# Seven block products in place of eight for the second FFN's input, and its width in three parts

## The chip, the cores and the metric

The kernel runs on one core of a Trainium2 chip. TensorE (PE) multiplies, VectorE (DVE) and ScalarE (ACT) do elementwise work, GpSimd (POOL) a few small operations, and SyncE (SP) issues the weight transfers. Each engine works through its own instructions in program order, and semaphores order the engines against each other. The metric is the device time of one execution in microseconds (us).

## The reference, cut to what matters

Two transformer blocks run one after the other on a sequence of 256 tokens with 2048 channels, in float32. What the change touches is the second block's feed-forward network, of width 5632:

```python
def conv_ffn(h, w_ffn_in, conv_w, conv_b, w_ffn_out):
    S = h.shape[1]
    up = h @ w_ffn_in                               # 2048 x 11264
    a, b = up[..., :D_FF_2], up[..., D_FF_2:]       # D_FF_2 = 5632
    a_pad = jnp.pad(a, ((0, 0), (CONV_W - 1, 0), (0, 0)))
    a = (conv_w[0] * a_pad[:, 0:S] + conv_w[1] * a_pad[:, 1:S + 1]
         + conv_w[2] * a_pad[:, 2:S + 2] + conv_b)
    return (jax.nn.gelu(a, approximate=True) * b) @ w_ffn_out
```

The input h is the RMS-normed row, and the output gets an RMS norm of its own and is added to x. The first block has a gated network of the same width (silu(g) * u), without the convolution.

## The kernel before, in words

**Products.** Each float32 weight and activation is split in two parts, high and low (`hi`, `lo`), and a product is three matmuls: high by high, high by low, low by high. A weight block is 128 x 1024: two contraction tiles of 128 by one group of 512 columns. `Sched` streams the blocks in one fixed order through all stages: SP loads a block into one of 4 raw buffers (`wraw`, L92), ACT writes its high part (`whi`, L113), DVE the low part (`wlo`, L115), each into one of 5 buffers. `take` hands the next block to PE; it first loads up to 6 blocks ahead (`LEAD_DMA`) and splits up to 4 ahead (`LEAD_SPLIT`). `q.tick()` follows each block and runs what was put off by a number of ticks (`later`, `step_of`) and a step of the background work (`q.work`).

**V tasks.** A group of 512 output columns takes 8 blocks of 12 matmuls with 512 moving columns (L1261 to L1263): 96 matmuls. The second FFN's input before is such tasks alone: group j of the convolved half, then group 11+j of the other half, for j from 0 to 10. We call the two a pair, of 192 matmuls. The first one (`by_tile`) runs the two halves of the tokens one after the other. Each group is evacuated by `f2_evac`: ACT scales the two accumulators into `ab`; two ticks later PE transposes 8 blocks of 128 x 128 (L465) into two PSUM tiles `m`. For the convolved half `conv` follows on each tile (two ACT operations at L1107, four of DVE through the helper at L283, then `gelu` on ACT); for the other half `gated` multiplies on DVE and `act_split` writes the high part on ACT and the low part on DVE.

**S tasks.** The first FFN's input runs in pairs already (`pairs_of_groups`, `pair_products`, products in the helper `three`, L1286 to L1288). Eight contraction pairs c are gone through in the order `ORDER`. Five of them take their two blocks as they are, 24 matmuls. For the three in `SEVEN` a 2 x 2 block product is formed with 7 products in place of 8 (21 matmuls): their blocks go out as left, sums1, sums2, right. The two sums blocks are made by DVE from the left and the right raw block with four operations (L145 to L149) and split like any other, so the raw buffers of both stay taken until then. The sums of the activations (`comb`) are made once beforehand, by `combine`. At the last of the sevens DVE builds four partial results from the four extra PSUM tiles (`u`, `g`), and each of the accumulators is added to one of them.

**Order and space.** All is written in program order by `Sched`; no planner reorders it. Activations, `hx4`, `x1`, `ff`, `act` and others live in 15 slots of 8 KB per partition (`slot`). The second FFN's width is worked through in the two parts of `PARTS`: groups 0 to 5, then 6 to 10. After each part the output product `w_f2o` (V tasks) adds that part's share to `ff` in `f_out`; in the last part group 3 of the output is run by the task `W` with 256 moving columns, in two halves, and the end of it is the end of the kernel: `f_tile`, `out_row`, and the stores.

Of the kernel before, what the change touches and what calls it, by code (L numbers as in the profile page):

```python
# [19 lines left out]
S = 256  # L20
# [6 lines left out]
PARTS = ((0, 6), (6, NG))  # L27
A_HEADS = 8
# [200 lines left out]
def body(ctx, tc, A, out):  # L229
# [149 lines left out]
    def pairs_of_groups(arr, of, order, lhs, comb, gate, done, first):  # L379

        blks = [b for x, y in of for b in pair_blocks(arr, x, y, order)]
        tasks.append(("S", blks, (len(of), order, lhs, comb, gate, done, first)))
# [4 lines left out]
    st = {}  # L387
# [79 lines left out]
    def turned(key, f0, srcs, use=None, then=None, gain=None, wait=2, comb=()):  # L467

        def part(j):
            def fn():  # L470
                m = mtile()
# [22 lines left out]
    def combine(key, i, m, gain):  # L494

        y, s = t512("y"), t512("s4")
        for n in range(2):
            copy(y[:, cols(n, S)], m[:, cols(n, S)], gain[n])
        a11, a21, a12, a22 = [y[:, cols(n, P)] for n in range(4)]
# [7 lines left out]
        halves(st[("comb", key)][i // 2][:, i % 2], s)  # L507

# [263 lines left out]

    for a, b in PARTS:
        C(lambda n=b - a: new_h("act", n))
        pairs_of_groups(A["w_f1"], [(j, NG + j) for j in range(a, b)], ORDER, rhs_of("hx2"), comb_of("hx2"), n1, "act",
                        (b - a) % 2)
# [352 lines left out]
    def f2_evac(key, j, use, then):  # L1129
        def evac(accs):  # L1130
            turned(key, 4 * j, scaled("ab", accs, n3), use, then)
        return evac

# [7 lines left out]
    def f_out(g, part):  # L1141
        def evac(accs):
            for k in range(2):
                y = st["ff"][k][:, cols(g)]
                if part == 0:
                    copy(y, accs[k])
                else:
                    out_sum(accs[k], k, g, cols(g))
            if part:
# [38 lines left out]
    def start_ff():  # L1188
        st["ff"] = [slot([P, D], name="ff") for _ in range(2)]
        st["post"] = slot([P, D], name="post")  # L1190
# [99 lines left out]
    def turn_act(key, f0, rows, tile):  # L1290
        for j in range(2):
            m = tile()
            turn(m, rows, j)
            f = f0 + 2 * j
            h_tile(key, f)
            dst = st[key][f // 4][:, f % 4:f % 4 + 2]
            split(dst[:, :, 0], dst[:, :, 1], pairs(m))

    def pair_products(count, order, lhs, comb, norm, key, first):
# [4 lines left out]
        prev = None  # L1304
        for n in range(count):
            own, shared = (acc_tile, mtile) if (n + first) % 2 == 0 else (mtile, acc_tile)
            for i, (c, seven) in enumerate(order):
# [30 lines left out]
                else:  # L1338
# [29 lines left out]
        turned(key, 4 * (count - 1), prev)  # L1368

# [112 lines left out]
def _layout(a):  # L1482
# [28 lines left out]
    r["w_f2os"] = _wblk(a["w_ffn_out_2"][0], range(4 * PARTS[1][0], 4 * NG))  # L1511
# [20 lines left out]
```

## Time and profile before

| what | value |
|---|---|
| time, median of 3 runs | 2739.64 us (2739.2 to 2743.42) |
| profiled execution, its own time | 2742.58 us |
| its span, first to last instruction | 2740.8 us |
| busy: PE, DVE, ACT | 2708.5 us (99%), 1689.7 us (62%), 1355.4 us (49%) |
| first FFN's input, S tasks | 851 to 1110 us and 1275 to 1460 us |
| second FFN's input, V tasks | about 1984 to 2265 us and 2396 to 2623 us |

Times inside the profile are us from the start of the span. A PE matmul's shown duration overlaps with the next one, so what a matmul costs is the distance from its start to the start of the next, and a busy PE need not be PE at its peak. Idle time stands in brackets ahead of what ended it.

### The profile page before, as it was taken

Reading aid. Unit: us, or ns where it says so; the run is one execution under the profiler, and the core shown is the slowest. Engines: PE = TensorE matmul, PEld = TensorE weight load, DVE = VectorE, ACT = ScalarE, POOL = GpSimd, SP = SyncE. Lnnn points to the kernel's source line nnn. Section 1 sums busy time; section 2 is a strip of 40 time slices with the busy share of each in tenths; the row PEclk is TensorE's granted clock in tenths of the full one; section 3 lists DMA queues with packets and bytes.
Section 4 is the critical chain, followed back from the end, with each engine's and each line's share of the span. In section 5 each row is a group of like instructions: output and inputs, shape, how many; then the busy total and the mean of one; then the engine's idle time right before and its main releaser. Section 6 shows DMA issues by size and latency. Waiting matters only on the chain.

```text
span 2740.8 us, 33567 instructions
## 1 busy us (share of the span) xinstructions
PE 2708.5 (99%) x12777; PEld 2253.2 (82%) x12777; DVE 1689.7 (62%) x2033; ACT 1355.4 (49%) x1759; POOL 59.5 (2%) x61
## 2 busy tenths in 40 slices
PE   8999999999999999999999999999999999999998
PEld 7888788888888887888888888888778888888887
DVE  5456555554467898648886557775555554455555
ACT  5445444444455555435555455554455554455543
POOL 0000000000000000000000001110000000000000
PEclk9999999999999999999999999999999999999999
DMA  8554456555555555655656565445555555555554
GB/s 276 175 181 163 160 171 215 194 189 196 191 177 195 179 200 191 209 194 182 207 184 204 183 210 168 145 152 191 177 177 184 185 185 191 192 191 185 185 189 142
DMA packets 142227, 511.42 MB, mean 187 GB/s; under 512 B 16945, under 2 KB 17329, under 8 KB 141553
## 3 DMA queue, kind: packets, MB, share of 16 engines
q1 hardware_dynamic: 140832, 502.71, 55.6%
q0 software_dynamic: 1088, 6.55, 0.6%
q8 instruction: 100, 1.64, 0.2%
q14 instruction: 63, 0.51, 0.1%
q10 hardware_dynamic: 144, 0.01, 0.0%
HBM read 507.11 MB, written 2.10 MB: 186 GB/s over the span
## 4 chain that ended last, share of the span: by engine, by line
PE 82%; DVE 8%; DMA 4%; issue 3%; ACT 2%; POOL 0%; DVEq 0%; ACTq 0%; POOLq 0%
PE acc L1263 21%; PE acc L1261 21%; PE acc L1262 21%; PE acc L1388 8%; DVE wlo L115 4%; PE acc L1390 4%; DMA wraw<-in_w_f 3%; PE m L465 1%; ACT whi L113 1%; DVE u L277 1%; PE acc L1286 1%; PE acc L1287 1%; PE acc L1288 1%; DVE sums L145 1%; DVE sums L146 1%
## 5 line engine op out<-in xcount | busy, mean ns | idle before, releaser
L115 DVE TENSOR_TENSOR wlo<-wraw,whi 128x1024 fp32r<-128x1024 f32 (+1 forms) x934 | 1119.3, 1206 | 802.6 <-ACT whi L113 798.7
L113 ACT ACTIVATE whi<-wraw 128x1024 fp32r<-128x1024 f32 (+1 forms) x934 | 966.6, 1041 | 788.3 <-PE acc L1263 675.0
L1261 PE MATMUL acc<-whi,hx 128*128 128x512 f32 x1456 | 581.7, 400 | 7.1 <-ACT hx L274 5.3
L1262 PE MATMUL acc<-wlo,hx 128*128 128x512 f32 x1456 | 568.4, 390 | 1.2 <-DVE wlo L115 1.2
L1263 PE MATMUL acc<-whi,hx 128*128 128x512 f32 x1456 | 569.3, 391 | 0.0
L1388 PE MATMUL acc<-hx,whi 128*128 128x512 f32 x912 | 330.6, 404 | 0.0
L1261 PEld LDWEIGHTS acc<-whi,hx 128*128 128x128 f32 x1456 | 274.0, 188 | 64.3 <-ACT hx L274 5.3
L1262 PEld LDWEIGHTS acc<-wlo,hx 128*128 128x128 f32 x1456 | 274.2, 188 | 58.8 <-DVE wlo L115 2.4
L1263 PEld LDWEIGHTS acc<-whi,hx 128*128 128x128 f32 x1456 | 273.8, 188 | 58.5
L1261 PE MATMUL acc<-whi,act 128*128 128x512 f32 (+1 forms) x704 | 271.1, 385 | 0.0
L1263 PE MATMUL acc<-whi,act 128*128 128x512 f32 (+1 forms) x704 | 269.8, 383 | 0.0
L1262 PE MATMUL acc<-wlo,act 128*128 128x512 f32 (+1 forms) x704 | 269.8, 383 | 0.0
L1390 PE MATMUL acc<-hx,wlo 128*128 128x256 f32 x912 | 255.7, 280 | 0.0
L1388 PEld LDWEIGHTS acc<-hx,whi 128*128 128x128 f32 x912 | 171.3, 188 | 38.9 <-issue 0.5
L1390 PEld LDWEIGHTS acc<-hx,wlo 128*128 128x128 f32 x912 | 172.4, 189 | 1.0 <-issue 0.5
L1263 PEld LDWEIGHTS acc<-whi,act 128*128 128x128 f32 x704 | 132.3, 188 | 26.1
L1261 PEld LDWEIGHTS acc<-whi,act 128*128 128x128 f32 x704 | 132.3, 188 | 25.7
L1262 PEld LDWEIGHTS acc<-wlo,act 128*128 128x128 f32 x704 | 132.4, 188 | 25.4
L113 ACT ACTIVATE whi<-sums 128x1024 fp32r<-128x1024 f32 x66 | 68.9, 1057 | 112.6 <-DVE sums L146 72.9
L1286 PE MATMUL m<-whi,hx 128*128 128x512 f32 x291 | 113.8, 391 | 0.0
L1288 PE MATMUL m<-whi,hx 128*128 128x512 f32 x291 | 113.3, 389 | 0.0
L1287 PE MATMUL m<-wlo,hx 128*128 128x512 f32 x291 | 113.3, 389 | 0.0
(332 smaller groups left out, 3047.9 us busy)
## 6 DMA issues: line engine op xcount, KB each, us to landing
wraw<-in_w_f SPq DMA_DIRECT2D x352, 512.0 KB, 3.4
wraw<-in_w_f1o SPq DMA_DIRECT2D x88, 512.0 KB, 4.2
wraw<-in_w_f2o SPq DMA_DIRECT2D x78, 512.0 KB, 3.3
wraw<-in_w_ga SPq DMA_DIRECT2D x34, 512.0 KB, 3.3
wraw<-in_w_vr SPq DMA_DIRECT2D x32, 512.0 KB, 3.3
wraw<-in_w_gr SPq DMA_DIRECT2D x32, 512.0 KB, 3.3
wraw<-in_w_gret SPq DMA_DIRECT2D x32, 512.0 KB, 3.9
wraw<-in_w_or SPq DMA_DIRECT2D x32, 512.0 KB, 3.3
```

The lines of the kernel that those rows point to most:

```text
L113: nc.scalar.activation(hi[:, c], raw[:, c], AF.Copy)
L115: nc.vector.tensor_tensor(lo[:, c], raw[:, c], hi[:, c].bitcast(F32), op=ALU.subtract)
L145: tt(t1, b12, b11, op=ALU.subtract)
L146: tt(t3, b22, b12, op=ALU.subtract)
L1261: nc.tensor.matmul(accs[k], x[:, 0], hi[:, w], start=b, stop=False)
L1262: nc.tensor.matmul(accs[k], x[:, 0], lo[:, w], start=False, stop=False)
L1263: nc.tensor.matmul(accs[k], x[:, 1], hi[:, w], start=False, stop=e)
L1286: nc.tensor.matmul(acc, x[:, 0], hi, start=start, stop=False)
L1287: nc.tensor.matmul(acc, x[:, 0], lo, start=False, stop=False)
L1288: nc.tensor.matmul(acc, x[:, 1], hi, start=False, stop=stop)
L1388: nc.tensor.matmul(acc, hi[:, w], x.rearrange("p a b -> p (a b)"), start=(k == first), stop=False, skip_group_check=True)
L1390: nc.tensor.matmul(acc[:, S:], lo[:, w], x[:, 0], start=False, stop=(k == last), skip_group_check=True)
```

## The change

The second FFN's input becomes S tasks too, for ten of its eleven pairs; pair 0 stays as two V tasks. A new order `ORDER_2` places the three sevens at 3, 5 and 6 of 8, the last two next to each other. `hx4` is not kept unsplit, so `combine_later` adds its two halves again and forms the sums, one step per tick, starting in the second V task of pair 0. What follows a pair is put into classes: `Gated` for the first FFN does what stood in `pair_products` before, except that the last pair's transposes go into the accumulators' own PSUM tiles; `Convolved` adds the accumulators to the partial results on DVE (`rows`), scales on ACT, and calls `turned` with `conv` or `gated` as before. The width is worked through in three parts (`PARTS_2`: groups 0 to 3, 4 to 7, 8 to 10), so `f_out` runs once more and the task `W` has 12 contraction tiles in place of 20, with its `out_row` calls placed anew. `ffn_post_norm_2` is loaded ahead of the last part's output and not of the first's. The sums slot of the first FFN is given back after it (`free_sums`).

```diff
+PARTS_2 = ((0, 4), (4, 8), (8, NG))
...
+    def combine_later(key, cs):
+        for i, c in enumerate(cs):
+            y = t512("y")
+            x = st[key][c // 2][:, 2 * c % 4:2 * c % 4 + 2].bitcast(F32)
+            tt(pairs(y), x[:, :, 0], x[:, :, 1], ALU.add)
+            yield
+            sums_of(key, i, y)
+            yield
...
+    class Convolved:
+        def last(self, n, shared):
+            pass
+
+        def rows(self, accs, y):
+            for k in range(2):
+                tt(y[k], accs[k], y[k], ALU.add)
+            for k in range(2):
+                copy(y[k], y[k], n3.r[:, k:k + 1])
+
+        def left(self, n, accs, g, own):
+            self.rows(accs, g)
+            turned("conv", 4 * (self.j0 + n), g, conv(self.f0), gelu, tile=own)
+
+        def right(self, n, accs, u, own):
+            self.rows(accs, u)
+            turned("act", 4 * (self.j0 + n), u, gated, act_split, tile=own)
...
+    ORDER_2 = [(3, False), (4, False), (0, True), (5, False), (1, True), (2, True), (6, False), (7, False)]
+    end = PARTS_2[-1][0]
-    for a, b in PARTS:
+    for a, b in PARTS_2:
         C(lambda n=b - a: (new_h("act", n), new_h("conv", 0)))
-        for j in range(a, b):
-            if j:
-                V(A["w_f2"], j, hx4, f2_evac("conv", j - a, conv(4 * a), gelu))
-            else:
-                by_tile(A["w_f2"], 0, hx4, first_tile, x4_hooks)
-            V(A["w_f2"], NG + j, hx4, f2_evac("act", j - a, gated, act_split))
         if a == 0:
-            C(start_ff)
-        for g in range(4 if a == 0 else 3):
+            by_tile(A["w_f2"], 0, hx4, first_tile, x4_hooks)
+            C(lambda: q.work[0].append(combine_later("hx4", SEVEN)))
+            V(A["w_f2"], NG, hx4, f2_evac("act", 0, gated, act_split, acc_tile))
+        js = range(max(a, 1), b)
+        pairs_of_groups(A["w_f2"], [(j, NG + j) for j in js], ORDER_2, hx4, comb_of("hx4"),
+                        Convolved(4 * a, js[0] - a), len(js) % 2)
+        C(start_ff if a == 0 else load_post if a == end else lambda: None)
+        for g in range(4 if a < end else 3):
             V(A["w_f2o"], g, lambda k, a=a: rhs_of("act", 5)(k - 4 * a), f_out(g, a), cs=range(2 * a, 2 * b))
-    W(A["w_f2os"], range(4 * PARTS[1][0], 4 * NG), lambda k: act_row(k - 4 * PARTS[1][0]), f_last, f_tile,
-      {(1, g): [(out_row, 0, g)] for g in range(4)})
+    W(A["w_f2os"], range(4 * end, 4 * NG), lambda k: act_row(k - 4 * end), f_last, f_tile,
+      {(1, 0): [(out_row, 0, 0)], (1, 1): [(out_row, 0, 1), (out_row, 0, 2)], (1, 2): [(out_row, 0, 3)]})
```

In `pair_products` the code after the last block of a pair's left and right half becomes:

```diff
                     if e:
-                        if prev is not None:
-                            turn_act(key, 4 * (n - 1), prev, shared)
-                        for k, acc in enumerate((c11, c21)):
-                            tt(g[k], acc, g[k], ALU.add)
-                        for k in range(2):
-                            nc.scalar.activation(g[k], g[k], AF.Silu, scale=norm.r[:, k:k + 1])
+                        after.last(n, shared)
+                        after.left(n, (c11, c21), g, own)
...
                     if e:
-                        for k, acc in enumerate((c12, c22)):
-                            tt(u[k], acc, u[k], ALU.add)
-                        for k in range(2):
-                            stt(g[k], u[k], norm.r[:, k:k + 1], g[k], ALU.mult, ALU.mult)
-                        prev = g
+                        after.right(n, (c12, c22), u, own)
```

## Rows read from the trace of the kernel before

**Rows 1.** The page: busy us, share of the span, instructions.

```profile
PE 2708.5 (99%) x12777; PEld 2253.2 (82%) x12777; DVE 1689.7 (62%) x2033; ACT 1355.4 (49%) x1759; POOL 59.5 (2%) x61
```

**Rows 2.** Stretches: start:end, length, busy time per engine (instructions), clock, DMA share, GB/s.

```profile
976.04:1019.45 43.41, 43.00 (x192) 35.02 (x191) 38.97 (x48) 23.89 (x28) 0.00 (x0) 1.00 0.56 194
1019.45:1062.59 43.14, 42.79 (x193) 35.02 (x192) 38.97 (x47) 23.13 (x27) 0.00 (x0) 1.00 0.58 195
2083.52:2128.97 45.45, 45.45 (x209) 37.60 (x208) 25.65 (x29) 23.64 (x28) 0.00 (x0) 1.00 0.57 184
```

**Rows 3.** PE timeline in a V task: start, length, engine, line, instruction, count.

```profile
2037.83 0.39 PE L1263 MATMUL acc<-whi,hx 128*128 128x512 f32 x1
2038.06 0.60 PE L465 MATMUL m<-c_ident,ab 128*128 128x128 f32 x4
2038.42 0.48 PE L1261 MATMUL acc<-whi,hx 128*128 128x512 f32 x1
2038.73 0.40 PE L1262 MATMUL acc<-wlo,hx 128*128 128x512 f32 x1
```

**Rows 4.** DVE timeline of an S pair: [idle before it, and what ended that].

```profile
1022.80 1.28 DVE L277 TENSOR_TENSOR act<-acc,act 128x512 fp32r<-128x512 f32 x2
1024.00 1.28 DVE L277 TENSOR_TENSOR g<-m,g 128x512 f32<-128x512 f32 x2
...
1027.03 1.23 DVE L115 TENSOR_TENSOR wlo<-sums,whi 128x1024 fp32r<-128x1024 f32 x1 [0.43 <-ACT whi L113]
...
1029.37 1.40 DVE L283 SCALAR_TENSOR_TENSOR g<-u,r_x,g 128x512 f32<-128x512 f32 x2
1030.70 1.22 DVE L115 TENSOR_TENSOR wlo<-sums,whi 128x1024 fp32r<-128x1024 f32 x1
1031.83 2.96 DVE L115 TENSOR_TENSOR wlo<-wraw,whi 128x512 fp32r<-128x512 f32 x3
1035.93 0.69 DVE L145 TENSOR_TENSOR sums<-wraw 128x512 f32<-128x512 f32 x1 [1.14 <-DMA wraw<-in_w_f]
...
1046.03 0.69 DVE L145 TENSOR_TENSOR sums<-wraw 128x512 f32<-128x512 f32 x1 [1.04 <-DMA wraw<-in_w_f]
...
1052.14 4.09 DVE L115 TENSOR_TENSOR wlo<-wraw,whi 128x512 fp32r<-128x512 f32 x4
1057.48 1.22 DVE L115 TENSOR_TENSOR wlo<-wraw,whi 128x1024 fp32r<-128x1024 f32 x1 [1.25 <-ACT whi L113]
```

**Rows 5.** Waits of SP's own queue, 851 to 1110: us in total, times, longest.

```profile
SPq L92 <- DVE wlo L115: 137.4, 79, 7.1
```

**Rows 6.** PE timeline in an S pair, sums1 of the last seven.

```profile
1031.23 0.39 PE L1286 MATMUL m<-whi,comb 128*128 128x512 f32 x1
1031.97 0.50 PE L1287 MATMUL m<-wlo,comb 128*128 128x512 f32 x1 [0.35 <-DVE wlo L115]
```

**Rows 7.** Stretch of one V pair, instructions on the tile cv alone: DVE, ACT.

```profile
2083.52:2128.97 45.45, 6.43 (x12) 4.46 (x8) 1.00 0.57 184
```

**Rows 8.** ACT and DVE timelines: a silu pair, the convolution's ACT pair and DVE four.

```profile
1024.71 1.34 ACT L1351 ACTIVATE g<-g,r_x 128x512 f32<-128x512 f32 x2 [3.54 <-DVE g L277]
...
2106.88 1.02 ACT L1107 ACTIVATE cv<-m,c_conv_b,c_conv_w 128x256 f32<-128x256 f32 x2 [1.52 <-PE m L465]
...
2107.93 1.91 DVE L283 SCALAR_TENSOR_TENSOR cv<-m,c_conv_w,cv 128x255 f32<-128x255 f32 x4 [1.32 <-ACT cv L1107]
```

**Rows 9.** The end: two matmuls of W on PE, then DVE.

```profile
2716.79 0.28 PE L1262 MATMUL acc<-wlo,act 128*128 128x256 f32 x1
2716.91 0.28 PE L1263 MATMUL acc<-whi,act 128*128 128x256 f32 x1
...
2724.79 0.42 DVE L277 TENSOR_TENSOR ff<-acc,ff 128x256 f32<-128x256 f32 x1 [3.97 <-PE acc L1263]
...
2726.98 2.74 DVE L283 SCALAR_TENSOR_TENSOR ff<-ff,r_f,x 128x512 f32<-128x512 f32 x4 [0.45 <-POOL r_f L419]
2731.99 0.42 DVE L277 TENSOR_TENSOR ff<-acc,ff 128x256 f32<-128x256 f32 x1 [2.26 <-PE acc L1263]
```

More of the change, by code (lines that the diff above doesn't have):

```diff
@@ L377, in pair_blocks, with pairs_of_groups @@
         return blks
-    def pairs_of_groups(arr, of, order, lhs, comb, gate, done, first):
+    def pairs_of_groups(arr, of, order, lhs, comb, after, first):
         blks = [b for x, y in of for b in pair_blocks(arr, x, y, order)]
-        tasks.append(("S", blks, (len(of), order, lhs, comb, gate, done, first)))
+        tasks.append(("S", blks, (len(of), order, lhs, comb, after, first)))
     def C(fn):
@@ L465, in turn, with turned @@
                 nc.tensor.transpose(m[:, (i * len(srcs) + k) * P:][:, :P], src[:, (n * j + i) * P:][:, :P], ident)
-    def turned(key, f0, srcs, use=None, then=None, gain=None, wait=2, comb=()):
+    def turned(key, f0, srcs, use=None, then=None, gain=None, wait=2, comb=(),
+               tile=mtile):
         def part(j):
             def fn():
-                m = mtile()
+                m = tile()
                 turn(m, srcs, j)
@@ L494, in combine, with sums_of @@
     def combine(key, i, m, gain):
-        y, s = t512("y"), t512("s4")
+        y = t512("y")
         for n in range(2):
             copy(y[:, cols(n, S)], m[:, cols(n, S)], gain[n])
+        sums_of(key, i, y)
+    def sums_of(key, i, y):
+        s = t512("s4")
         a11, a21, a12, a22 = [y[:, cols(n, P)] for n in range(4)]
@@ L507, in combine @@
         halves(st[("comb", key)][i // 2][:, i % 2], s)
+    def combine_later(key, cs):
+        for i, c in enumerate(cs):
+            y = t512("y")
+            x = st[key][c // 2][:, 2 * c % 4:2 * c % 4 + 2].bitcast(F32)
+            tt(pairs(y), x[:, :, 0], x[:, :, 1], ALU.add)
+            yield
+            sums_of(key, i, y)
+            yield
     def comb_of(key):
@@ L770, in body, with turn_act, free_sums, __init__ @@
         V(A["w_out"], g, rhs_of("mg"), row_add("hx2", g, n1, "norm_ffn", SEVEN))
+    def turn_act(f0, rows, tile):
+        for j in range(2):
+            m = tile()
+            turn(m, rows, j)
+            f = f0 + 2 * j
+            h_tile("act", f)
+            dst = st["act"][f // 4][:, f % 4:f % 4 + 2]
+            split(dst[:, :, 0], dst[:, :, 1], pairs(m))
+    def free_sums():
+        q.mixed = None
+    class Gated:
+        def __init__(self, count):
+            self.count = count
+        def last(self, n, shared):
+            if n:
+                turn_act(4 * (n - 1), self.rows, shared)
+        def left(self, n, accs, g, own):
+            for k in range(2):
+                tt(g[k], accs[k], g[k], ALU.add)
+            for k in range(2):
+                nc.scalar.activation(g[k], g[k], AF.Silu, scale=n1.r[:, k:k + 1])
+            self.rows = g
+        def right(self, n, accs, u, own):
+            g = self.rows
+            for k in range(2):
+                tt(u[k], accs[k], u[k], ALU.add)
+            for k in range(2):
+                stt(g[k], u[k], n1.r[:, k:k + 1], g[k], ALU.mult, ALU.mult)
+            if n == self.count - 1:
+                turned("act", 4 * n, g, tile=own)
     for a, b in PARTS:
         C(lambda n=b - a: new_h("act", n))
-        pairs_of_groups(A["w_f1"], [(j, NG + j) for j in range(a, b)], ORDER, rhs_of("hx2"), comb_of("hx2"), n1, "act",
-                        (b - a) % 2)
+        pairs_of_groups(A["w_f1"], [(j, NG + j) for j in range(a, b)], ORDER, rhs_of("hx2"), comb_of("hx2"),
+                        Gated(b - a), (b - a) % 2)
+        if a:
+            C(free_sums)
         if a:
@@ L1127, in act_split, with f2_evac, __init__, last @@
         split(dst[:, :, 0], dst[:, :, 1], pairs(st.pop(("cv", f))))
-    def f2_evac(key, j, use, then):
+    def f2_evac(key, j, use, then, tile=mtile):
         def evac(accs):
-            turned(key, 4 * j, scaled("ab", accs, n3), use, then)
+            turned(key, 4 * j, scaled("ab", accs, n3), use, then, tile=tile)
         return evac
+    class Convolved:
+        def __init__(self, f0, j0):
+            self.f0, self.j0 = f0, j0
+        def last(self, n, shared):
+            pass
+        def rows(self, accs, y):
+            for k in range(2):
+                tt(y[k], accs[k], y[k], ALU.add)
+            for k in range(2):
+                copy(y[k], y[k], n3.r[:, k:k + 1])
+        def left(self, n, accs, g, own):
+            self.rows(accs, g)
+            turned("conv", 4 * (self.j0 + n), g, conv(self.f0), gelu, tile=own)
+        def right(self, n, accs, u, own):
+            self.rows(accs, u)
+            turned("act", 4 * (self.j0 + n), u, gated, act_split, tile=own)
     st["first"] = []
@@ L1146, in evac @@
                     copy(y, accs[k])
+                elif part < PARTS_2[-1][0]:
+                    tt(y, accs[k], y, ALU.add)
                 else:
                     out_sum(accs[k], k, g, cols(g))
-            if part:
+            if part == PARTS_2[-1][0]:
                 yield "pre"
@@ L1189, in start_ff, with load_post @@
         st["ff"] = [slot([P, D], name="ff") for _ in range(2)]
+    def load_post():
         st["post"] = slot([P, D], name="post")
         nc.gpsimd.dma_start(st["post"], A["ffn_post_norm_2"])
[L1193 removed]
+    ORDER_2 = [(3, False), (4, False), (0, True), (5, False), (1, True), (2, True), (6, False), (7, False)]
+    end = PARTS_2[-1][0]
+    for a, b in PARTS_2:
         C(lambda n=b - a: (new_h("act", n), new_h("conv", 0)))
[L1195 to L1203 removed]
+        if a == 0:
+            by_tile(A["w_f2"], 0, hx4, first_tile, x4_hooks)
[6 more added lines that the diff above has]
+        for g in range(4 if a < end else 3):
             V(A["w_f2o"], g, lambda k, a=a: rhs_of("act", 5)(k - 4 * a), f_out(g, a), cs=range(2 * a, 2 * b))
[L1205 to L1206 removed]
+    W(A["w_f2os"], range(4 * end, 4 * NG), lambda k: act_row(k - 4 * end), f_last, f_tile,
+      {(1, 0): [(out_row, 0, 0)], (1, 1): [(out_row, 0, 1), (out_row, 0, 2)], (1, 2): [(out_row, 0, 3)]})
     blocks = [b for t in tasks for b in t[1]]
@@ L1288, in three, with pair_products @@
         nc.tensor.matmul(acc, x[:, 1], hi, start=False, stop=stop)
[L1290 to L1299, printed above, removed]
+    def pair_products(count, order, lhs, comb, after, first):
         sevens = [i for i, (c, seven) in enumerate(order) if seven]
-        prev = None
         for n in range(count):
@@ L1510, in _layout @@
     r["w_f2o"] = _vblk(a["w_ffn_out_2"][0])
-    r["w_f2os"] = _wblk(a["w_ffn_out_2"][0], range(4 * PARTS[1][0], 4 * NG))
+    r["w_f2os"] = _wblk(a["w_ffn_out_2"][0], range(4 * PARTS_2[-1][0], 4 * NG))
     for n in ("attn_post_norm_2", "ffn_post_norm_2"):
```

1 line of the change is left out of this document (removed).

## The prediction, made before the changed kernel was run

> **What bounds the kernel now.** I read the page first: PE is busy for 99% of the span, DVE for 62%, ACT for 49% [rows 1]. That is an average over stages, so I went on to the stretches of the two kinds of task, one pair each. A V pair takes 45.45 us with PE busy throughout and DVE at 25.65 us [rows 2]: PE alone sets its length. An S pair of the first FFN takes 43.14 us with DVE at 38.97 us [rows 2]. PE needs less than that. Four transposes cost 0.44 us (0.67 us from their start to the second matmul after them, less 0.23 us for the one matmul between [rows 3]). A V pair has four such sets, so a matmul costs (45.45 - 1.76) / 192 = 0.2275 us. An S pair of the first FFN has 183 matmuls and two sets, 42.5 us; the 0.6 us above that are stalls, such as the second matmul of sums1 waiting for its low part from DVE [rows 6].
>
> The DVE timeline says why DVE is late with 10% of its time free. In one S pair it stands still four times, 3.86 us together [rows 4]. Two of these waits are for a raw block to land before sums1 (1.14 and 1.04), one is for the high part of the last block of the pair (1.25), one for the high part of a sums block that is queued behind silu on ACT (0.43). Busy and idle make 38.97 + 3.86 = 42.83 us, near the whole period of 43.14. The raw waits are DVE's own doing: SP's queue waits almost only for DVE's low parts to free a raw buffer [rows 5]. DVE frees a buffer, the transfer follows, and DVE itself needs the block three operations later. So the first FFN's pairs already run at the pace of a loop through DVE, SP and the transfer, with PE 0.6 us behind its own limit. The question for the change is what this loop comes to when the convolution's work is put into it.
>
> **What the change takes from PE.** Three sevens save 3 matmuls each: 9 x 0.2275 = 2.05 us per pair. The transposes stay. PE's own limit for a pair falls from 45.45 to 43.40 us.
>
> **What it gives to DVE.** I start from the 38.97 us of the S pair. The two gate products (1.33 us from their start to the next operation) and the two low parts of the activations (1.20 us) [rows 4] belong to the first FFN and go. In their place come all of DVE's operations on the tile cv, 6.43 us in a V pair [rows 7]: eight of the convolution, two products, two low parts. The additions to the partial results are the same in both. That makes 38.97 - 1.33 - 1.20 + 6.43 = 42.87 us, against 25.65 us in the V pair and under PE's 43.40 by a mere 0.5.
>
> **The waits inside it.** One by one, in the new program order:
> - The wait before sums1 of contraction pair 1 stays, 1.14 us. Between the low part that frees the buffer (right block of pair 0) and sums1 there are again two low parts, as in the row of three low parts ahead of that wait [rows 4].
> - The wait before sums1 of pair 2 goes (1.04): with pair 1 right ahead of it, its buffers are freed by pair 5's low parts, six DVE operations and 6 us earlier.
> - The wait for the last block of the pair stays, 1.25 us: its buffer is freed by the last seven's right block, three low parts ahead, as before [rows 4].
> - The wait behind silu goes (0.43).
> - A new one comes. After the right half DVE adds two accumulators; next in its queue are the four operations of the convolution. They wait for ACT's pair, and ACT has the two scalings of the right half first. From the start of the first addition: 0.7 us until ACT can start, 1.34 for two scalings (the silu pair is the nearest row), 1.02 for the convolution's pair [rows 8], 3.0 in all; DVE is free after 1.2 [rows 4]. That is 1.8 us of standing still. In the V task the same four wait 1.32 us [rows 8], but there DVE had time. Bounds: 0, if the wait fell into one that is there anyway, and 3.0. Behind it in DVE's queue are the sums and low part for the first seven, so it delays all that follows. I take 1.8.
>
> The loop is then 42.87 + 1.14 + 1.25 + 1.8 = 47.06 us, above PE's 43.40 and above the V pair's 45.45. The same tally gave 0.3 too little for the first FFN. PE would stand still about 3.6 us per pair: for the transposes of the left half, whose rows DVE adds late, and in the last seven.
>
> **Summed over the parts.** The parts have 3, 4 and 3 S pairs. The first pair of a part starts with four blocks split and no convolution from a pair before it, so PE sets its pace: 183 x 0.2275 = 41.6 us, then 0.4 waiting for the left half's rows and 0.44 for their transposes, 42.4. Each further pair costs the loop, 47.1. The other three sets of transposes of the last pair fall into the output product, 1.3. Three pairs: 42.4 + 2 x 47.1 + 1.3 = 137.9 against 3 x 45.45 = 136.35, +1.55. Four: 185.0 against 181.8, +3.2. All together 1.55 + 3.2 + 1.55 = +6.3 us.
>
> **The rest of the change.**
> - The task W loses 8 contraction tiles, 96 matmuls of 0.12 us [rows 9], and the V tasks of the output gain 48 of 0.2275: 11.5 less 10.9, a gain of 0.6.
> - At the end, tile 1's last products now come 36 x 0.12 = 4.3 us after tile 0's in place of 7.2 (2724.79 to 2731.99 for the first addition after each [rows 9]). Tile 0's four output rows end at 2726.98 + 2.74, 4.9 us after its first addition [rows 9]. They stand ahead of tile 1's addition in DVE's queue, so the end is 0.6 later. The two cancel.
> - `combine_later` puts some 7 us of DVE work (15 additions and three splits, an estimate from 0.6 us per 512 columns [rows 4]) into the V task and the first S pair of part 0. In a V task DVE has 45.45 - 25.65 = 19.8 us free per pair: nothing, and where that cover failed, at most the 7.
> - The third `f_out` adds two DVE operations per group in V tasks, hidden in the same slack. Without it, 1.2 us for each of four groups.
> - Slots: `x1` 2, `hx4` 4, sums of `hx4` 2, sums of weights 1, `ff` 2 and `act` 4 fill all 15. The next part's `act` takes those whose readers are done. Moving the load of `ffn_post_norm_2` puts 1 MB on POOL's queue, which is otherwise idle there. I cost both at nothing; a raw block landing late by the 1 to 2 us of such a meeting is the bound.
>
> Forecast: +6.3 us. On the profiled execution's own 2742.58 us (span 2740.8 and 1.8 around it) that is 2748.9. This execution is 2.9 us above the median of the runs; on the median, 2739.64, it is 2746.0, slower by 0.23%. What a measurement of this kernel can tell from no change is about 0.2%, 5.5 us, so the forecast lies at that edge.
>
> **Rivals.**
> *The waits overlap and PE sets the pace.* DVE's 42.87 us fit under PE's 43.40. If the four waits fall together, every pair gains 2.05: ten pairs, -20.5, 2719. If half of the 4.2 us of waiting stays, the loop is 45.0, and by the same sum the parts give -2.7, -3.1 and -2.7: -8.5, 2731. For it: V pairs with PE busy throughout [rows 2]. Against it: in the first FFN DVE has 3.5 us to spare under PE's 42.5, and still stalls it [rows 6], because each wait follows from DVE's own freeing and not from PE. The Trainium skill (Perfetto Trace Analysis, Identifying the Most-Contended Engine) takes the engine with the highest occupancy as the most contended one, with occupancy a fair measure for VectorE; by that rule PE stays the bound, and this rival's 2719 would follow. The trace of the first FFN speaks against reading it so: there the occupancy of DVE is 90% [rows 2] and the loop still sets the period.
>
> *The second half of the convolution waits too.* In DVE's order it comes after the first seven's sums and a low part, 2.3 us after the first half; ACT needs a gelu (0.67, half of the silu pair) and its own pair of 1.02 [rows 8] in that time, so it fits by about 0.6, if PE has done the transposes. From the point where PE is more than 2 us behind the left half's rows, it doesn't, and another wait of up to 1.8 us comes in each of the seven pairs that run in the loop: +12.6, 2758.6. For it: in the V pair the first half's four wait for exactly this ACT pair [rows 8].
>
> *The width's three parts cost by themselves,* by a slot or transfer that comes late at one of two new seams: a few us each, within the range above 2746.
>
> **How the numbers follow.** The loop as summed, with the pair between 46.5 and 47.7 (+2 to +11): 0.60, its own range 2742 to 2751. Overlapping waits, 2717 to 2737: 0.25. The second wait or seams, 2751 to 2760: 0.15. The range that leaves out about 2 in 10 is 2724 to 2755. Slower by over 0.2% (above 2745.1): over half of the loop's share and near all of the last, 0.43. Within 0.2%: the rest of the loop's share and the edge of the first rival's, 0.33. Faster: 0.24.
>
> **What will show it.** Right: in the second and third S pair of a part, DVE's period is near 47 us with about 42.9 busy; its rows show one wait of some 1.8 us ahead of the convolution, one for a raw block at the fifth place of the order and none at the sixth, and one at the last block; PE waits for the scaled rows at the left half's transposes. The first pair of each part takes some 42 us. Wrong: a period near 43.4 with PE busy throughout, or a DVE that is busy for much less than 42.9, or a long stall at a part's start.

## The result, and the profile after

The changed kernel takes 2772.34 us (median, 2771.41 to 2773.53) against 2739.42 us on the same chip: a ratio of 1.0117, 95% interval 1.0099 to 1.0134. It is slower, as forecast, but by 32.9 us in place of 6.3, and the time lies 17 us above the range.

The page of the changed kernel (profiled execution 2771.74 us, span 2770.0 us) answers to [rows 1]: 138 matmuls fewer, 177 us more of DVE's time.

```profile
PE 2710.2 (98%) x12639; PEld 2237.4 (81%) x12639; DVE 1866.9 (67%) x2319; ACT 1401.4 (51%) x1832; POOL 59.9 (2%) x61
```

PE's busy time did not fall with its instructions (2708.5 before; the shown duration of a matmul includes its wait for the one before), so the page does not place the loss. The starts of PE's instructions at the edges of the stages do. The span grew by 29.2 us:

| stage | before | after | difference | forecast |
|---|---|---|---|---|
| up to the first FFN | | | -0.7 | 0 |
| first FFN, both parts | 718.8 | 724.4 | +5.6 | 0 |
| pair 0 of the second FFN | 54.0 | 56.8 | +2.8 | 0 |
| its ten other pairs | 453.5 | 470.9 | +17.4 | +2.4 |
| its output products | 242.8 | 246.4 | +3.6 | +3.9, less W's 0.6 |
| tail after the last matmul | 9.13 | 9.68 | +0.6 | +0.6 |

The ten pairs take 44.54, 48.56, 48.69 in the first part, 42.40, 48.54, 50.24, 48.36 in the second, 42.37, 48.77, 48.43 in the third. The first pairs of the second and third part are the 42.4 us of the forecast. The later ones are near 48.5 in place of 47.1.

**One later pair, DVE.** The stretch of the second pair (columns as in [rows 2], the engines in the order PE, PEld, DVE, ACT, POOL; PEld is PE's weight loads), then its DVE timeline with all four waits of the pair; the first row is the pair of additions that opens it.

```profile
2087.60:2136.16 48.56, 45.58 (x203) 35.55 (x201) 42.27 (x54) 28.01 (x36) 0.00 (x0) 1.00 0.52 175
```

```profile
2085.19 1.28 DVE L278 TENSOR_TENSOR g<-m,g 128x512 f32<-128x512 f32 x2
2088.23 1.23 DVE L116 TENSOR_TENSOR wlo<-wraw,whi 128x1024 fp32r<-128x1024 f32 x1 [1.75 <-ACT whi L114]
2089.37 1.28 DVE L278 TENSOR_TENSOR u<-m,u 128x512 f32<-128x512 f32 x2
2092.36 1.91 DVE L284 SCALAR_TENSOR_TENSOR cv<-m,c_conv_w,cv 128x255 f32<-128x255 f32 x4 [1.71 <-ACT cv L1163]
...
2108.49 0.69 DVE L146 TENSOR_TENSOR sums<-wraw 128x512 f32<-128x512 f32 x1 [1.20 <-DMA wraw<-in_w_f]
...
2115.20 0.68 DVE L146 TENSOR_TENSOR sums<-wraw 128x512 f32<-128x512 f32 x1
...
2126.56 1.23 DVE L116 TENSOR_TENSOR wlo<-wraw,whi 128x1024 fp32r<-128x1024 f32 x1 [1.17 <-ACT whi L114]
```

Here are 42.27 us of work and 1.75 + 1.71 + 1.20 + 1.17 = 5.83 of waiting, 48.10 of the 48.56. This sum by itself shows no loop: an engine's work and its idle time fill any stretch, and DVE's 25.65 us of work and its waits fill the V pair of 45.45 [rows 2] as well, where PE sets the pace. What shows it is that a wait taken out shortens the pair (experiments 2, 3 and 5). Three waits are those of the forecast: 1.71 ahead of the convolution (1.8 taken), 1.20 for a raw block at the first of the adjacent sevens (1.14) and none at the second, at 2115.20, 1.17 at the last block (1.25). The first wait, 1.75, was in no step. ACT's timeline at the same place says what it is:

```profile
2085.91 1.34 ACT L275 ACTIVATE g<-g,r_x 128x512 f32<-128x512 f32 x2 [2.24 <-DVE g L278]
2087.15 1.04 ACT L114 ACTIVATE whi<-wraw 128x1024 fp32r<-128x1024 f32 x1
2090.09 1.33 ACT L275 ACTIVATE u<-u,r_x 128x512 f32<-128x512 f32 x2 [1.89 <-DVE u L278]
2091.33 1.00 ACT L1163 ACTIVATE cv<-m,c_conv_b,c_conv_w 128x256 f32<-128x256 f32 x2
```

DVE adds the left half; ACT waits for that, scales it, and then makes the high part of the next block, which is next in its queue. DVE has that block's low part next and waits for both. Then the same passage again: DVE adds the right half, ACT scales it, and then runs the convolution's pair, for which DVE waits.

**The first FFN's seam.** Two stretches, the output products of its parts, answered in the changed kernel by 134.87 and 118.95 us where the kernel before has 132.30 and 113.56. First the kernel before, then the changed one, whose third row is a piece of its second:

```profile
1110.17:1242.47 132.30, 131.71 (x585) 108.66 (x583) 70.59 (x68) 53.97 (x53) 0.00 (x0) 1.00 0.60 194
1456.35:1569.91 113.56, 112.93 (x513) 93.00 (x511) 63.62 (x68) 53.86 (x69) 0.00 (x0) 1.00 0.60 193
```

```profile
1108.91:1243.78 134.87, 131.73 (x585) 108.65 (x583) 70.67 (x68) 54.07 (x53) 0.00 (x0) 1.00 0.58 191
1455.92:1574.87 118.95, 115.78 (x512) 95.00 (x511) 63.85 (x68) 53.95 (x69) 0.00 (x0) 0.97 0.55 184
1463.00:1468.20 5.20, 5.20 (x14) 4.00 (x13) 2.44 (x3) 1.54 (x2) 0.00 (x0) 0.50 0.50 150
```

PE's timeline there, changed kernel, shows the transposes of the last S pair waiting for the rows that DVE makes:

```profile
1114.59 0.33 PE L466 MATMUL m<-c_ident,g 128*128 128x128 f32 x1 [2.81 <-DVE g L284]
...
1458.42 0.39 PE L1348 MATMUL acc<-whi,act 128*128 128x512 f32 x1
1461.78 0.47 PE L466 MATMUL m<-c_ident,g 128*128 128x128 f32 x1 [2.98 <-DVE g L284]
1463.58 0.63 PE L1347 MATMUL acc<-wlo,act 128*128 128x512 f32 x1
1464.00 0.63 PE L1348 MATMUL acc<-whi,act 128*128 128x512 f32 x1
```

Before, `turned("act", ...)` for the last pair was called after the loop over the pairs; now `Gated.right` calls it inside, before the last tick of the loop. `turned` waits two ticks, so the transposes come one block earlier in PE's queue, and the gate products are not done yet. PE stands still for them. After the second stand the granted clock is 0.50 (1.2 in place of 2.4 GHz), matmuls start 0.42 us apart, and 11 of them do so before it is 1.00 again. The two stretches are 2.6 and 5.4 us longer than before, 8.0 together; the S parts ahead of them are 2.3 us shorter, so that 5.6 is left in the table.

### The profile page after: what moved, and what is told of

The parts are those of the page before. It is cut to its first block, busy times and chain, and to the rows that moved or that the text cites. A ratio compares the mean times of both kernels' runs of the same rounds, so it can differ in the third digit from the quotient of the medians.

```text
span 2770.0 us, 33717 instructions
## 1 busy us (share of the span) xinstructions
PE 2710.2 (98%) x12639; PEld 2237.4 (81%) x12639; DVE 1866.9 (67%) x2319; ACT 1401.4 (51%) x1832; POOL 59.9 (2%) x61
## 5 line engine op out<-in xcount | busy, mean ns | idle before, releaser
L116 DVE TENSOR_TENSOR wlo<-wraw,whi 128x1024 fp32r<-128x1024 f32 (+1 forms) x936 | 1098.9, 1188 | 652.5 <-ACT whi L114 648.3
L114 ACT ACTIVATE whi<-wraw 128x1024 fp32r<-128x1024 f32 (+1 forms) x936 | 948.9, 1026 | 667.1 <-PE acc L1348 493.0
L1346 PE MATMUL acc<-whi,hx 128*128 128x512 f32 x816 | 329.8, 404 | 6.7 <-ACT hx L275 5.2
L1347 PE MATMUL acc<-wlo,hx 128*128 128x512 f32 x816 | 320.1, 392 | 0.7 <-DVE wlo L116 0.7
L1348 PE MATMUL acc<-whi,hx 128*128 128x512 f32 x816 | 320.0, 392 | 0.0
L1346 PE MATMUL acc<-whi,act 128*128 128x512 f32 (+1 forms) x704 | 274.2, 390 | 0.0
L1348 PE MATMUL acc<-whi,act 128*128 128x512 f32 (+1 forms) x704 | 272.5, 387 | 0.0
L114 ACT ACTIVATE whi<-sums 128x1024 fp32r<-128x1024 f32 x126 | 132.6, 1059 | 190.1 <-DVE sums L147 113.6
L1372 PE MATMUL m<-wlo,hx 128*128 128x512 f32 x579 | 226.6, 391 | 1.6 <-DVE wlo L116 1.6
L1371 PE MATMUL m<-whi,hx 128*128 128x512 f32 x579 | 227.8, 393 | 0.0
L1373 PE MATMUL m<-whi,hx 128*128 128x512 f32 x579 | 225.9, 390 | 0.0
L1346 PEld LDWEIGHTS acc<-whi,hx 128*128 128x128 f32 x816 | 154.2, 189 | 39.9 <-ACT hx L275 5.2
L1347 PEld LDWEIGHTS acc<-wlo,hx 128*128 128x128 f32 x816 | 154.5, 189 | 34.6 <-DVE wlo L116 2.1
L1348 PEld LDWEIGHTS acc<-whi,hx 128*128 128x128 f32 x816 | 154.3, 189 | 33.1
L1372 PE MATMUL acc<-wlo,hx 128*128 128x512 f32 x450 | 176.0, 391 | 2.1 <-DVE wlo L116 2.1
L1371 PE MATMUL acc<-whi,hx 128*128 128x512 f32 x450 | 176.5, 392 | 0.0
L1373 PE MATMUL acc<-whi,hx 128*128 128x512 f32 x450 | 175.4, 390 | 0.0
```

The costliest lines, as they stand in the source:

```text
L114: nc.scalar.activation(hi[:, c], raw[:, c], AF.Copy)
L116: nc.vector.tensor_tensor(lo[:, c], raw[:, c], hi[:, c].bitcast(F32), op=ALU.subtract)
L1346: nc.tensor.matmul(accs[k], x[:, 0], hi[:, w], start=b, stop=False)
L1347: nc.tensor.matmul(accs[k], x[:, 0], lo[:, w], start=False, stop=False)
L1348: nc.tensor.matmul(accs[k], x[:, 1], hi[:, w], start=False, stop=e)
L1371: nc.tensor.matmul(acc, x[:, 0], hi, start=start, stop=False)
```

## The experiments

The names are those of the expectations, where they have one. **Queue theory:** the later pairs are the sum of DVE's work and of waits in series, each made by a passage DVE to ACT and back or DVE to SP to transfer and back; the seam is a matter of one tick. **Rival A:** DVE simply has too much work (42.3 us in a loop whose other limit is 43.4), and waits shift when one is removed. **Rival B:** the rate of the weight transfers, or the PSUM tiles that the pairs now share, set the pace. **Rival C:** the three parts cost by themselves. Edits are against the changed kernel unless said otherwise. Ratios are to the kernel before, which took 2743.24 us beside experiments 1 to 4 and 2743.16 beside 5 to 8.

**1. The first FFN's transposes one tick later.**

```diff
             if n == self.count - 1:
-                turned("act", 4 * n, g, tile=own)
+                turned("act", 4 * n, g, tile=own, wait=3)
```

> The changed kernel with one edit: at the end of the first FFN's last pair of each part the transposes are put off by three ticks in place of two, as before the change. Queue theory (each stall follows from the program order of DVE and ACT and from DVE's own freeing of raw buffers): the second FFN's pairs stay at 48.5 us each; at the two places where the first FFN's output begins PE stood 2.96 and 3.13 us and, after the second, ran 11 matmuls at half clock (2.2 us); these go back to about 0.4 each, so about 7 us less: 2765. Rival (the seam is a side show and moves elsewhere, since DVE is late by the same work): 2771 to 2772, with the stall at a later transposition.

2768.42 us (2767.09 to 2770.37; 2765 expected), ratio to the kernel before 1.0094 (1.0079 to 1.0109); span 2765.8, 4.2 less. The two stretches of the output products, and PE's stand ahead of the first transpose:

```profile
1110.04:1242.50 132.46, 131.72 (x585) 108.66 (x584) 70.71 (x68) 53.97 (x53) 0.00 (x0) 1.00 0.58 194
1454.82:1568.39 113.57, 112.93 (x512) 93.00 (x511) 63.60 (x68) 53.84 (x69) 0.00 (x0) 1.00 0.59 193
```

```profile
1116.05 0.33 PE L466 MATMUL m<-c_ident,g 128*128 128x128 f32 x1 [0.40 <-DVE g L284]
```

Both are back at the lengths of before, 7.8 us less, and no half clock is left there (1.00 in the second). The seam's mechanism stands. Not all of it reached the span: at the last transposes of pair 0 the kernel is still 7.4 us ahead (2039.2 in place of 2046.6), at the first ones of the first S pair 5.9 (2080.9 in place of 2086.8), with a granted clock of 0.55 between 2040 and 2043, and 4.2 at the end. The last 1.7 are spread over the later pairs of the second FFN, each up to 0.4 longer in this execution than in the changed kernel's; why was not followed.

**2. The scaling off the passage.** ACT scales the four partial results before the last contraction pair's products; the additions become one DVE operation per accumulator that scales and adds.

```diff
+        def early(self, g, u):
+            for y in (g, u):
+                for k in range(2):
+                    copy(y[k], y[k], n3.r[:, k:k + 1])
+
         def rows(self, accs, y):
             for k in range(2):
-                tt(y[k], accs[k], y[k], ALU.add)
-            for k in range(2):
-                copy(y[k], y[k], n3.r[:, k:k + 1])
+                stt(y[k], accs[k], n3.r[:, k:k + 1], y[k], ALU.mult, ALU.add)
...
                 else:
+                    if e:
+                        after.early(g, u)
                     if b:
                         c11, c21 = own(), own()
```

> The changed kernel with the scaling of a pair's rows taken out from between DVE's additions and what follows: ACT scales the four partial results ahead of the last contraction pair's additions, and DVE adds scaled accumulators in one operation (accumulator times scale plus partial result). Same count of operations on both engines. Queue theory: the waits of 1.75 us (a low part whose high part is queued on ACT behind the scaling of the left half) and of 1.71 us (the convolution behind the scaling of the right half) go, DVE's four operations cost 0.24 more: the pairs after the first of a part go from 48.5 to about 45.3, and the kernel by some 3.2 x 7 plus 2 in the first pair's end, to 2748. Rival A (DVE's plain load sets the pace, waits only fill up): the pairs stay at 48 or above, 2770. Rival B (the weight transfers or the PSUM tiles that the pairs now share set the pace): no change, 2772.

2751.72 us (2750.0 to 2755.56), ratio 1.0033 (1.002 to 1.0046); span 21.8 less than the changed kernel's. Later pairs take 44.9 to 46.2 us (one 47.1; 45.3 expected). A pair's stretch, and DVE where the two waits of ACT had been:

```profile
2313.50:2359.70 46.20, 44.52 (x201) 35.71 (x200) 42.99 (x56) 28.02 (x36) 0.00 (x0) 1.00 0.56 181
```

```profile
2355.99 1.40 DVE L284 SCALAR_TENSOR_TENSOR g<-m,r_x,g 128x512 f32<-128x512 f32 x2
2357.67 1.23 DVE L116 TENSOR_TENSOR wlo<-wraw,whi 128x1024 fp32r<-128x1024 f32 x1 [0.28 <-ACT whi L114]
2358.81 1.40 DVE L284 SCALAR_TENSOR_TENSOR u<-m,r_x,u 128x512 f32<-128x512 f32 x2
2360.13 1.90 DVE L284 SCALAR_TENSOR_TENSOR cv<-m,c_conv_w,cv 128x255 f32<-128x255 f32 x4
```

DVE works more than in the changed kernel (42.99 for 42.27), and the pair is 2.4 shorter: 1.75 fell to 0.28, and 1.71 to nothing. That is against rival A, which expected 48 or above, and against rival B, which expected no change.

**3. A fifth raw buffer,** `RAW_BUFS = 5` in place of 4, which opens the loop through SP and the transfer.

> The changed kernel with five raw weight buffers in place of four. Queue theory: the waits of DVE for raw blocks (1.20 before sums1 of the first of the two adjacent sevens, 1.17 for the high part of the last block) go, so the second FFN's later pairs fall from 48.5 to about 46.2 (7 pairs, 16 us), and the first FFN's S pairs, whose three such waits make 3.4 us, fall from 43.1 to PE's 42.5 (8 pairs, 5 us): 2751. Rival A (DVE's load): 2770. Rival B (the rate of the transfers, not the number of buffers): no change, 2772.

2741.26 us (2739.16 to 2744.38), ratio 0.9997 (0.9987 to 1.0006). This gained 10 us more than expected. Of the 29.2 us by which the span fell, the ten pairs gave 21.7 (16 expected of them), the first FFN's S parts 4.7 (5 expected), and the stretches between the rest. Later pairs 45.3 to 46.0 (46.2 expected); the first FFN's S parts, 257.99 and 211.69 in the changed kernel, became 254.18 and 210.83. One pair, and the only two waits of DVE in it:

```profile
2302.40:2348.40 46.00, 44.72 (x202) 35.65 (x200) 42.09 (x54) 27.89 (x36) 0.00 (x0) 1.00 0.54 175
```

```profile
2303.01 1.22 DVE L116 TENSOR_TENSOR wlo<-wraw,whi 128x1024 fp32r<-128x1024 f32 x1 [1.76 <-ACT whi L114]
...
2307.15 1.91 DVE L284 SCALAR_TENSOR_TENSOR cv<-acc,c_conv_w,cv 128x255 f32<-128x255 f32 x4 [1.71 <-ACT cv L1163]
```

42.09 + 1.76 + 1.71 = 45.56 of 46.00: exactly the waits that a buffer can answer went, the others did not move. The two that went made 2.37 us, and the pair is 2.6 shorter. The Trainium skill (Perfetto Trace Analysis, Optimization Strategy) says that one gap repeating on the engine that should be saturated can mean too few buffers for the next tile; the 1.20 and 1.17 of the pair above, which come in every later pair at about this size (one is 2.63) and are gone with the fifth buffer, agree.

**4. The kernel before with three parts,** which is the `PARTS_2` part of the change alone (not shown below: `f_out`, the load of `ffn_post_norm_2` and the `out_row` calls, changed with it).

```diff
+PARTS_2 = ((0, 4), (4, 8), (8, NG))
...
-    for a, b in PARTS:
+    for a, b in PARTS_2:
```

> The kernel before with the width in three parts alone, the second FFN's input still in V tasks. All theories: the task W loses 96 matmuls of 0.12 us for 48 of 0.2275 (0.6 less), the end comes 0.6 later by tile 0's output rows: 2739.5, within 1 us of before. A rival that puts part of the loss on the seams of the three parts expects 2742 to 2750.

2743.09 us (2740.57 to 2744.99) against 2743.24 there, ratio 0.9998 (0.9989 to 1.0008): no difference. Rival C falls.

**5. All three repairs together:** the edits of 1, 2 and 3.

> The changed kernel with the three edits together: the first FFN's last transposes a tick later, the scaling ahead of the additions, five raw buffers. Queue theory: with both the ACT waits (3.46 us, less 0.24 for the dearer additions) and the raw waits (2.37) out of DVE's queue, a pair's loop is 48.5 - 3.2 - 2.4 = 42.9, and PE's own 43.4 sets the pace; ten pairs gain 2.05 each over V pairs, the first FFN's pairs another 4 to 5 in all: about 25 under the kernel before, 2715 where that is 2740. Rival A (DVE's load with some waits that always remain keeps the pair at 45 or above): 2735 to 2740, no better than five buffers alone.

2716.16 us (2716.01 to 2717.06), ratio 0.9901 (0.9884 to 0.9917): faster than both kernels. Later pairs 43.35 to 43.8; the first pairs of the second and third part 41.84, that of the first part 44.06. One later pair, and the page:

```profile
2333.30:2376.70 43.40, 43.40 (x203) 36.02 (x201) 42.75 (x55) 28.12 (x35) 0.00 (x0) 1.00 0.60 200
```

```profile
PE 2686.6 (99%) x12639; PEld 2238.2 (82%) x12639; DVE 1869.6 (69%) x2319; ACT 1408.7 (52%) x1832; POOL 59.9 (2%) x61
```

The pair takes the 43.40 us that the prediction worked out for PE alone, with DVE at 42.75 inside it and PE without a gap. This is the run that decides between the queue theory and rival A: the same work on DVE, 0.2 us of waits, and PE sets the pace. In the span the three repairs alone took 4.2, 21.8 and 29.2 us, 55.2 in sum; together they took 55.6. Waits in series add up so; that the two agree to 0.4 is partly luck, since executions of one of these kernels lie up to 6 us apart.

**6. The fifth raw buffer in the kernel before.**

> The kernel before with five raw buffers. Queue theory: the first FFN's S pairs lose their waits for raw blocks and go from 43.1 to PE's 42.5, 4 to 5 us in all; V pairs stay at 45.45, for PE sets them: 2735 where before is 2740. A rival (the transfers have slack by the number of buffers everywhere): more than 8 us less.

2735.63 us (2734.28 to 2736.45), ratio 0.997 (0.9959 to 0.9981). That is 7.5 us less, more than the 4 to 5 expected and just under the 8 of the rival. The trace says where they are: the first FFN's S parts are 4.4 and 2.6 us shorter, and V pairs stay at 45.45. So the gain is not everywhere; it is about 0.6 us for each of the first FFN's eleven pairs, of which I had reckoned with fewer (eight in the text of experiment 3). PE is busy all through the first FFN's first S part:

```profile
851.14:1105.30 254.16, 254.16 (x1146) 210.86 (x1145) 230.89 (x273) 147.58 (x167) 1.08 (x1) 1.00 0.61 200
```

So the reading of the kernel before, that its S pairs already run behind the raw buffers' loop, holds. It also gives a fair base for experiment 5: the change with its repairs is worth 0.9901 / 0.997 = 0.993, some 19 us of 2736, and the ten pairs' 2.05 us of matmuls are 20.5. With the loop open, the products saved come out nearly whole.

**7. DVE's eight shifted terms taken out of the convolution,** so that DVE has some 3.3 us less to do in a pair (38.96 for 42.27; one execution).

```diff
-            for i in range(2):
-                y, x = c[:, cols(i, S)], m[:, cols(i, S)]
-                stt(y[:, 1:], x[:, :S - 1], cw[:, 1, f + i:f + i + 1], y[:, 1:], ALU.mult, ALU.add)
-                stt(y[:, 2:], x[:, :S - 2], cw[:, 0, f + i:f + i + 1], y[:, 2:], ALU.mult, ALU.add)
```

> The changed kernel without the two shifted terms of the convolution: the eight DVE operations per pair that follow ACT's first term are left out, so the output differs. DVE has 3.66 us less per pair, and what waited for ACT's pair is not there (1.71). Queue theory: the loop is 48.5 - 3.7 - 1.7 = 43.1, so the later pairs run at PE's 43.4 to 44. Rival A (load alone): 48.5 - 3.7 = 44.8. Rival B (transfers): 48.5.

2748.39 us, later pairs mostly 44.75 to 44.9. The queue theory as I had put it missed, with 43.4 to 44: I thought that the wait ahead of the convolution would go with the operations that stand in it. A pair, and two rows of DVE:

```profile
2310.10:2355.00 44.90, 44.00 (x202) 35.89 (x200) 38.96 (x46) 28.20 (x36) 0.00 (x0) 1.00 0.57 187
```

```profile
2310.67 1.23 DVE L116 TENSOR_TENSOR wlo<-wraw,whi 128x1024 fp32r<-128x1024 f32 x1 [1.75 <-ACT whi L114]
...
2315.75 1.23 DVE L116 TENSOR_TENSOR wlo<-wraw,whi 128x1024 fp32r<-128x1024 f32 x1 [1.46 <-ACT whi L114]
```

ACT's two scalings of the right half stand as much ahead of the next high part as of the convolution, so the next low part waits 1.46 in its stead. The wait belongs to the scalings, not to what follows them. The time alone is what rival A expected (44.8), so this run does not part it from the queue theory; experiment 5 does.

**8. The first FFN's order of the contraction pairs,** `ORDER` in place of `ORDER_2` (one execution).

```diff
-        pairs_of_groups(A["w_f2"], [(j, NG + j) for j in js], ORDER_2, hx4, comb_of("hx4"),
+        pairs_of_groups(A["w_f2"], [(j, NG + j) for j in js], ORDER, hx4, comb_of("hx4"),
```

> The changed kernel with the first FFN's order for the second FFN's pairs (sevens at 2, 4 and 6, none next to another). Queue theory: the wait of about 1.04 us before sums1 of the last seven comes back, and nothing else goes, so the later pairs take 49.5 or somewhat more (the sums of the first seven now stand two blocks nearer to the convolution): 2777 to 2785. Rival (two sevens next to each other are the harm, since their sums come faster than DVE can make them): the pairs get faster than 48.5.

2771.41 us, the changed kernel's time. I expected it slower, at 2777 to 2785, with later pairs of 49.5 or more. They take 46.8 to 50.2, and six of the seven are below 48.5, as the rival expected; their mean is 47.8, against 48.8 in the changed kernel. The first pair of the first part takes 48.17 in place of 44.54, which gives back more than half; in all the ten pairs are 2.5 us shorter, and other stages lose that again (not followed). A pair, and DVE at the place where the changed kernel waits 1.75:

```profile
2320.13:2368.17 48.04, 44.58 (x203) 35.77 (x201) 42.44 (x55) 28.36 (x36) 0.00 (x0) 1.00 0.53 175
```

```profile
2317.72 1.28 DVE L278 TENSOR_TENSOR g<-acc,g 128x512 f32<-128x512 f32 x2
2318.92 0.68 DVE L149 TENSOR_TENSOR sums<-wraw,sums 128x512 f32<-128x512 f32 x1
2319.64 0.69 DVE L150 TENSOR_TENSOR sums<-wraw,sums 128x512 f32<-128x512 f32 x1
2320.76 1.23 DVE L116 TENSOR_TENSOR wlo<-sums,whi 128x1024 fp32r<-128x1024 f32 x1 [0.43 <-ACT whi L114]
...
2328.47 1.91 DVE L284 SCALAR_TENSOR_TENSOR cv<-acc,c_conv_w,cv 128x255 f32<-128x255 f32 x4 [0.54 <-ACT cv L1163]
```

The 0.43 of [rows 4] is back, with ACT scaling where it ran silu before. Between the additions and the low part the old order has two operations on the sums, 1.3 us, and they cover the passage through ACT. `ORDER_2` has no seven at that place, the low part follows at once, and 0.43 became 1.75. The old order gains 1.3 us here. Part of it is lost on the second half of the convolution, which waits 0.54 for ACT in every later pair and in none of the changed kernel. The wait that I expected back ahead of the last seven's sums (1.04) did not come: one wait for a raw block is there, 1.14, as in the changed kernel. So the shorter pairs come from the order of DVE's queue after the left half; that adjacent sevens are the harm, as the rival has it, is not shown. In time the old order repairs nothing.

## Why the prediction was wrong, step by step

**Right.** The mechanism and the sign (slower had a chance of 0.43): the later pairs run at the pace of a loop through DVE and not of PE (5 shows the same work without the loop). The first pairs of the second and third part (42.40 and 42.37). The new wait ahead of the convolution (1.71 for 1.8), and the three statements on raw waits. The transposes in the output, W and the tail, which come to about +4 together (3.6 + 0.6 measured). Nothing for the three parts (4), and PE's own 43.40 (5). DVE's work was 42.27 for 42.87, 0.6 too much. One reading was too narrow, without an effect on the sum: SP does not wait almost only for low parts. The row below the one in [rows 5] has the sums operations, which free the raw buffers of the sevens; both are DVE's.

```profile
SPq L92 <- DVE sums L149: 81.8, 17, 5.7
```

**Wrong: "The wait behind silu goes (0.43)."** I read the row's releaser as silu and let the wait go with it. It belongs to any ACT operation between DVE's left additions and the next high part, and the row ahead of it, two operations on the sums, had covered 1.3 us of it. I had costed this passage for the right half, and not for the left half where it comes in the same way. It costs 1.75 in place of 0 in each of seven later pairs, 12 us of the 15 that the ten pairs took beyond the forecast. This was the step that decided: with it in the sum the forecast would have been 2746.0 + 12.2 = 2758, above the range.

**Wrong: the edit in `Gated` was costed at nothing.** I named the classes as a rearrangement (the section on the change says that `Gated` does what stood there before, which is not so) and did not count ticks. It moved the last transposes of the first FFN by one block: +8.0 us in the two stretches behind them, of which experiment 1 took back 7.8. By the rule that a moved step counts with everything it is moved past, this was to be seen in the diff: one call that stood behind the loop stood in it.

**Wrong: the first pair of the first part.** The forecast gave it 42.4 us like the others, with no convolution ahead of it. Pair 0 stands ahead of it, and PE's rows show eight transposes of pair 0's second group inside it, with two stands: 0.9 us of transposes and 0.9 of standing, most of the 2.1 that it takes beyond 42.4.

```profile
2046.56 0.33 PE L466 MATMUL acc<-c_ident,ab 128*128 128x128 f32 x1 [0.62 <-ACT ab L275]
2047.13 0.55 PE L466 MATMUL acc<-c_ident,ab 128*128 128x128 f32 x3 [0.25 <-ACT ab L275]
2050.28 0.60 PE L466 MATMUL acc<-c_ident,ab 128*128 128x128 f32 x4
```

**Not forecast: pair 0, +2.8 us.** PE stands 2.06 us ahead of its transposes (1.70 before), and 8 matmuls at half clock follow, some 8 x 0.2 = 1.6. The last 0.8 are a second stretch at half clock, earlier in the pair, where the kernel before had none (first row the changed kernel, second the kernel before):

```profile
1996.90:2001.20 4.30, 4.30 (x15) 3.46 (x14) 3.23 (x8) 3.17 (x9) 0.00 (x0) 0.60 0.66 225
1992.00:1996.30 4.30, 4.30 (x22) 3.29 (x20) 3.23 (x8) 3.02 (x9) 0.00 (x0) 1.00 0.68 223
```

Experiment 4, whose pair 0 is that of the kernel before, has such a stretch too and takes 54.8 us for the pair. So these 0.8 can come without the change.

**Not settled.** One pair is 50.24: its last raw block lands late, DVE waits 2.63 us there in place of 1.17, and a stand of PE of 2.19 us and a half clock follow. With five raw buffers the same pair takes 46.01; why the block is late there was not followed.

**The rivals.** Overlapping waits (2719, 20.5 us gained) did not come by themselves; it is about what came once the loop was opened, 19.5 us under the kernel before with the same buffers. The Trainium skill's rule of occupancy that stood with it (Perfetto Trace Analysis, Identifying the Most-Contended Engine) was read wrongly there: it judges TensorE not by its matmuls' busy share but by its share of peak throughput and by its weight loads. The weight loads take 35.55 us of the pair's 48.56, against DVE's 42.27, so by them the rule names DVE and not PE. The trace agrees that DVE is the place to look, but its work alone does not make the period: neither engine is full, and the waits fill it up. The second half of the convolution waited in no later pair (in the one shown its four start at 2096.53 without a gap); with the old order of experiment 8 it does, 0.54 us.

## What to carry to other kernels

Where an engine's queue alternates with another's, list its waits over one period and follow each back to what has to be done before the answer: if that is the waiting engine's own earlier work, the loop may be bound by waits in series. That work and waits together come to the period says nothing, for they always do. The proof is to take one wait out and see the period fall by about its length, as in experiments 2 and 3, until another engine sets the pace, as in 5. Each wait is priced by what stands in the other engine's queue ahead of the answer, less what covers it in the waiting engine's own. When work is put into such a loop, open it first (a further buffer, a scaling made early), and then the saved work shows. A call that moves into or out of a loop moves by its ticks, so count them even where the diff looks like tidying.

## What the runs showed of the hardware

After a short stand of PE (idle, waiting for rows to transpose) the granted clock fell to half, from 2.4 to 1.2 GHz, in some places and not in others, and the stand's length does not tell which: after 2.98 us (1461.78) and 2.19 us (2413.95) it was 0.50, after the 2.81 us at 1114.59 it was 1.00. Nor does the place: ahead of pair 0's first transposes PE stands for the same time in the changed kernel and with experiment 1's edit, first and second fence (PE's row, then the stretch behind it).

```profile
2023.67 0.33 PE L466 MATMUL m<-c_ident,ab 128*128 128x128 f32 x1 [2.06 <-ACT ab L275]
2024.90:2028.00 3.10, 3.10 (x8) 2.39 (x8) 2.02 (x5) 0.97 (x2) 0.00 (x0) 0.50 0.00 0
```

```profile
2016.38 0.33 PE L466 MATMUL m<-c_ident,ab 128*128 128x128 f32 x1 [2.07 <-ACT ab L275]
2017.60:2021.10 3.50, 3.50 (x19) 2.92 (x18) 2.40 (x7) 0.96 (x2) 0.00 (x0) 1.00 0.00 0
```

Eight matmuls in 3.1 us in the one, 19 instructions (four transposes among them) in 3.5 us in the other. In the second kernel the half clock comes 22 us later, in the first S pair. So a stand of 2 to 3 us may cost nothing more, or some 1.6 to 2.2 us more (8 to 11 matmuls at 0.42 in place of 0.23); what decides, no run here shows.
